# Modulation passes tied behind the linear attention's VectorE chain, and counted out anew

## The chip, the core and the metric

The kernel runs on one core of a Trainium2 chip. The metric is device time in microseconds of one execution. The engines are TensorE (PE in the profile, its weight loads PEld), VectorE (DVE), ScalarE (ACT), GpSimd (POOL) and SyncE (SP, whose DMA queue is SPq).

## What is computed

One step of a diffusion backbone with two layers over 512 latent and 128 context tokens (640 in all, 1,024 channels). Layer 0 mixes tokens with neighbourhood attention (A, 8 heads) beside bidirectional gated linear attention (B, 4 heads of key width 64 and value width 128), layer 1 with grouped-query attention; each layer ends in a gated feed-forward part. Every normalised input is scaled, shifted and gated by vectors of a modulation, one set for latent tokens and one for context tokens. The change lies in layer 0's mixer. Of the reference:

```python
def modulation(cvec, w, bias):
    mod = (jax.nn.silu(cvec) @ w + bias).reshape(-1, 1, 6 * D_MODEL)
    return jnp.split(mod, 6, axis=-1)

def gla_scan(q, k, v, g, s0):              # g = log alpha <= 0, chunks of tokens
    ...
    def step(s, inp):
        qc, kc, vc, gc = inp
        bcum = jnp.cumsum(gc.astype(jnp.float32), axis=2)
        o_inter = jnp.einsum('bhid,bhde->bhie', qc * jnp.exp(bcum).astype(qc.dtype), s)
        diff = bcum[:, :, :, None, :] - bcum[:, :, None, :, :]
        decay = jnp.exp(jnp.where(causal[:, :, None], diff, -jnp.inf)).astype(qc.dtype)
        att = jnp.einsum('bhid,bhjd,bhijd->bhij', qc, kc, decay)
        o = o_inter + jnp.einsum('bhij,bhje->bhie', att, vc)
        ...
        s_new = (jnp.exp(blast[:, :, 0, :])[..., None].astype(s.dtype) * s
                 + jnp.einsum('bhjd,bhje->bhde', k_dec, vc)).astype(s.dtype)
```

## The kernel before

Tokens lie along the free axis, channels along the partitions. A product of fp32 values is made of three matmuls over halves: a weight tile `ws` comes by DMA on SP's queue, its high half `wh` is a cast on ScalarE (L111), its low half `wl` a difference on VectorE or GpSimd (L112), and `step` (L155) multiplies `hh`, `hl` with `wh`, `wl` into `mm`; products with tokens on the partitions go into `tm` (L602 to L604), from which VectorE and ScalarE copy the values `v`. The `wh` pieces have six buffers.

Layer 0's mixer runs in this order on the chip: gates and scans of B, then the pieces of `ORDER` ("a0", "s0", "a1", "o0", "q0", "s1", "o1"), then A. Here 0 and 1 are the two pairs of heads, m in the code:

- "a" (`gla_scores`): decayed scores by levels. A level subtracts sums of gates into `ea` and `eb` (VectorE, L864 and L865), takes exponentials (ScalarE, L844), and multiplies by keys and queries (`ea` on GpSimd L870, `eb` on VectorE L871). 40 small matmuls (`lev`, L884) follow, which VectorE evicts through a mask (L889, into `acc` for the first of six levels; GpSimd adds the later ones to it). Two last levels go through `off` (L921), copied to `att` by ScalarE (L926, L927); eight VectorE copies (L930) put the diagonal blocks of `acc` into `att`.
- "s" (`gla_states`): decayed keys `kd` (ScalarE L948, GpSimd L949), transposed and copied to `kt`; `ds` (TensorE, L969), and the states `S` (VectorE, L974 and L975).
- "o" (`gla_out`): outputs `go` from `att`, `S` and decayed queries `qd`, copied to `got`.

Beside this, TensorE works through other products (values, the gate `rg`, A's first queries and keys), which `fill.some(n)` takes from a queue at fixed places. A's own keys of the context come as `kc` by DMA (SP, L801) and are split into `kch` (ScalarE) and `kcl` (VectorE); its first scores are `nas` (L1100).

The modulation's later vectors are made on VectorE from weights in `wa`: `modulations()` yields 48 steps in this stage, each a DMA of 256 KB into one of three `wa` buffers (SP, L323) and two multiply-and-add passes (L326, written to `junk` and, the second, over `wa` itself), 96 passes in all. `Fill.some(n, m)` also takes m of these steps. The numbers `SLEV`, `SOFF` and `SST` say how many are taken after a level, ahead of `off`, and ahead of each "s" and "o". An instruction's place on its engine is then set by a scheduler that builds one order for each engine; each engine works through its list in that order. `tc.issue_after(x)` is a condition on this order alone: what is issued within it stands behind x.

Of the kernel before, what the change touches and what calls it, by code (L numbers as in the profile page):

```python
# [12 lines left out]
ALU = mybir.AluOpType  # L13
# [7 lines left out]
NT = LAT + CTX  # L21
# [9 lines left out]
def kernel(ctx: ExitStack, tc: tile.TileContext, a: dict, o: dict):  # L31
# [205 lines left out]
    def run(gen):  # L237
        for _ in gen:
            pass

    class Fill:

# [17 lines left out]
        def some(self, n, m=0):  # L260
            while m and self.aside:
                m -= 1
                if next(self.aside[0], self) is self:
                    self.aside.pop(0)
            self.owed += n
            n = int(self.owed)
            self.owed -= n
            while n and self.queue:
                with tc.high_priority(offset=0):
                    end = next(self.queue[0], self) is self  # L270
                if end:
                    self.queue.pop(0)
                else:
                    n -= 1
                    self.newest = newest[0]
# [365 lines left out]
    def layer0(H, raws):  # L641
# [95 lines left out]
        for m, d in keys:  # L737
# [7 lines left out]
            last = nc.scalar.activation(ab, ab, AF.Exp, scale=-1.0)  # L745
            fill.some(RG1)
        with tc.issue_after(last.ins):
            for key in keys:
                last = nc.scalar.activation(logs[key], logs[key], AF.Ln, bias=1.0)
        for key in keys:  # L750
# [5 lines left out]
            else:  # L756
                nc.vector.tensor_tensor_scan(rev(c), gscan, rev(mins[key]), 0.0, ALU.mult, ALU.add)
            fill.some(RG2)


        with tc.issue_after(last.ins):
            S, OT, att = {}, {}, {}

            def piece(kind, m):
# [3 lines left out]
                elif kind == "s":  # L768
                    fill.until(g_vg)
                    fill.some(0, SST)  # L770
                    gla_states(m, kg[m], cum[m], vg, S, fill)
                elif kind == "o":
# [73 lines left out]
    def gla_scores(m, k, q, FG, fill):  # L846
        def level(h):
# [21 lines left out]
            if h > 1:  # L869
                nc.gpsimd.tensor_tensor(ea[:, 0:NT], ea[:, 0:NT], k[:, 0:NT], ALU.mult)  # L870
            nc.vector.tensor_tensor(eb[:, 0:NT], eb[:, 0:NT], q[:, 0:NT], ALU.mult)  # L871
            return ea, eb
# [51 lines left out]
        for e in range(2):  # L924
# [3 lines left out]
            for j in range(4):  # L928
                pj = slice(32 * j, 32 * j + 32)
                nc.vector.tensor_copy(  # L930
                    x[pj, 0:NT].rearrange("p (t i) -> p t i", i=128)[:, :, 32 * j:32 * j + 32],
# [5 lines left out]
    def gla_states(m, k, FG, vg, S, fill):  # L937
# [25 lines left out]
        for d, tiles in enumerate(order):  # L963
# [9 lines left out]
            for i, t in enumerate(tiles[0:3]):  # L973
                nc.vector.scalar_tensor_tensor(s[:, i + 1, :], s[:, i, :], dec[d][:, t:t + 1], ds[:, 128 * i:128 * i + 128], ALU.mult, ALU.add)  # L974
            nc.vector.tensor_copy(s[:, 4, :], ds[:, 384:512])  # L975
            nc.gpsimd.dma_start(o["gla"][d, m], s[:, 4, :])
# [536 lines left out]
RG1 = 6  # L1513
# [4 lines left out]
ROUT = 6  # L1518
SLEV = 2
SOFF = 4  # L1520
SST = 4
# [133 lines left out]
```

## Time and profile before

| | us |
|---|---|
| median of 3 runs | 1721.39 (1718.57 to 1723.66) |
| the profiled execution | 1717.48 |
| its span | 1715.7 |

TensorE is busy for 95% of the span, VectorE for 73%, ScalarE for 43% and GpSimd for 12%; TensorE's mean granted clock is 0.974 of full speed. Busy time is an average over stages: the first 260 us, in which layer 0's mixer makes B, look unlike the rest. Times below count from the span's start.

### The profile page before, as it was taken

Reading aid. Unit: us, or ns where it says so; the run is one execution under the profiler, and the core shown is the slowest. Engines: PE = TensorE matmul, PEld = TensorE weight load, DVE = VectorE, ACT = ScalarE, POOL = GpSimd, SP = SyncE. Lnnn points to the kernel's source line nnn. Section 1 sums busy time; section 2 is a strip of 40 time slices with the busy share of each in tenths; the row PEclk is TensorE's granted clock in tenths of the full one; section 3 lists DMA queues with packets and bytes.
Section 4 is the critical chain, followed back from the end, with each engine's and each line's share of the span. In section 5 each row is a group of like instructions: output and inputs, shape, how many; then the busy total and the mean of one; then the engine's idle time right before and its main releaser. Section 6 shows DMA issues by size and latency. Waiting matters only on the chain.

```text
span 1715.7 us, 33434 instructions
## 1 busy us (share of the span) xinstructions
PE 1635.8 (95%) x13142; PEld 1563.1 (91%) x13142; DVE 1258.2 (73%) x2767; ACT 742.4 (43%) x1681; POOL 208.9 (12%) x473
## 2 busy tenths in 40 slices
PE   7986988999999999999999999999999999999997
PEld 5886887879999999999998888889999999999997
DVE  5999865775999999986656987885876544663664
ACT  4443354453533323322335577775553322331342
POOL 2125541210200000000003310100100000000001
PEclk8998989999999999999998999999999999999999
DMA  8643332323354455453232200110222222222222
GB/s 320 206 136 103 103 103 81 95 87 105 100 163 155 146 174 184 146 158 110 72 122 88 69 20 14 50 56 31 70 82 79 62 76 75 81 71 82 73 70 68
DMA packets 68014, 175.22 MB, mean 102 GB/s; under 512 B 7920, under 2 KB 9744, under 8 KB 66832
## 3 DMA queue, kind: packets, MB, share of 16 engines
q1 hardware_dynamic: 67024, 171.48, 31.0%
q8 instruction: 103, 1.69, 0.4%
q0 software_dynamic: 832, 1.60, 0.3%
q14 instruction: 55, 0.45, 0.1%
HBM read 165.71 MB, written 7.34 MB: 101 GB/s over the span
## 4 chain that ended last, share of the span: by engine, by line
PE 79%; DVE 13%; ACT 3%; DMA 2%; issue 2%; POOL 1%; SPq 0%; ACTq 0%; DVEq 0%; POOLq 0%
PE mm L155 66%; DVE junk L326 2%; PE gpo L1339 2%; DVE wa L326 2%; PE gpt L1327 1%; DVE wl L112 1%; DMA wa<-in_ada_wt_dram 1%; PE gs L1318 1%; PE gs L1319 1%; DVE mx L1065 1%; PE ss L420 1%; PE tm L602 1%; PE napo L1131 1%; PE tm L604 1%; PE tm L603 1%
## 5 line engine op out<-in xcount | busy, mean ns | idle before, releaser
L155 PE MATMUL mm<-hh,wl 128*128 128x320 f32 x2080 | 652.3, 315 | 4.7 <-ACT rg L689 2.6
L155 PE MATMUL mm<-hl,wh 128*128 128x320 f32 x2080 | 648.2, 312 | 0.0
L155 PE MATMUL mm<-hh,wh 128*128 128x320 f32 x2080 | 641.5, 312 | 0.0
L111 ACT CAST wh<-ws 128x512 fp32r<-128x512 f32 x376 | 228.8, 615 | 438.2 <-PE mm L155 395.7
L155 PEld LDWEIGHTS mm<-hh,wl 128*128 128x128 f32 x2080 | 394.6, 190 | 14.7 <-issue 4.8
L155 PEld LDWEIGHTS mm<-hl,wh 128*128 128x128 f32 x2080 | 395.1, 190 | 2.6 <-issue 1.0
L155 PEld LDWEIGHTS mm<-hh,wh 128*128 128x128 f32 x2080 | 393.4, 190 | 0.4 <-issue 0.2
L112 DVE TENSOR_TENSOR wl<-ws,wh 128x512 fp32r<-128x512 f32 x348 | 243.5, 702 | 150.5 <-ACT wh L111 149.3
L155 PE MATMUL mm<-glo,wh 128*128 128x320 f32 x704 | 218.0, 310 | 0.0
L155 PE MATMUL mm<-ghi,wh 128*128 128x320 f32 x704 | 218.0, 311 | 0.0
L155 PE MATMUL mm<-ghi,wl 128*128 128x320 f32 x704 | 216.1, 311 | 0.0
L498 DVE SCALAR_TENSOR_TENSOR x<-mm,mod,x 128x192 f32<-128x192 f32 (+2 forms) x240 | 96.9, 435 | 88.8 <-PE mm L155 87.8
L155 PEld LDWEIGHTS mm<-ghi,wl 128*128 128x128 f32 x704 | 132.3, 189 | 1.3 <-issue 1.3
L155 PEld LDWEIGHTS mm<-glo,wh 128*128 128x128 f32 x704 | 133.1, 189 | 0.0
L155 PEld LDWEIGHTS mm<-ghi,wh 128*128 128x128 f32 x704 | 132.9, 189 | 0.1
L326 DVE SCALAR_TENSOR_TENSOR junk<-wa,sb 128x512 f32<-128x512 f32 x160 | 120.8, 760 | 7.2 <-DMA wa<-in_ada_wt_dram 6.9
L326 DVE SCALAR_TENSOR_TENSOR wa<-wa,sb 128x512 f32<-128x512 f32 x160 | 114.3, 721 | 0.3
L532 POOL MEMSET u<- 128x1 f32 x88 | 8.6, 100 | 760.9 <-DVE gate L525 426.3
L535 ACT COPY u<-mm 128x320 f32<-128x320 f32 x88 | 37.8, 431 | 87.7 <-PE mm L155 81.8
L602 PE MATMUL tm<-wl,hh 128*128 128x256 f32 x200 | 58.6, 300 | 8.0 <-ACT v L611 4.6
L1071 ACT ACTIVATE gp<-gs,mx,rq 128x640 f32<-128x640 f32 x64 | 57.1, 892 | 16.9 <-DVE mx L1067 11.6
L538 ACT COPY u<-mm 128x192 f32<-128x192 f32 x88 | 28.4, 323 | 79.7 <-PE mm L155 79.7
(302 smaller groups left out, 2436.6 us busy)
## 6 DMA issues: line engine op xcount, KB each, us to landing
ws<-in_wu_dram SPq DMA_DIRECT2D x88, 512.0 KB, 3.2
wa<-in_ada_wt_dram SPq DMA_DIRECT2D x160, 256.0 KB, 3.3
ws<-in_wd_dram SPq DMA_DIRECT2D x32, 448.0 KB, 3.5
aw<-in_ada_w_dram SPq DMA_DIRECT2D x8, 1024.0 KB, 14.7
ws<-in_w_ab_dram SPq DMA_DIRECT2D x16, 512.0 KB, 3.7
ws<-in_wd_dram SPq DMA_DIRECT2D x16, 512.0 KB, 3.5
x<-in_xT_dram SPq DMA_DIRECT2D x16, 320.0 KB, 3.0
ws<-in_w_gqa_dram SPq DMA_DIRECT2D x10, 512.0 KB
```

The lines of the kernel that those rows point to most:

```text
L111: nc.scalar.copy(hi, src)
L112: eng.tensor_tensor(lo, src, hi, ALU.subtract)
L155: newest[0] = nc.tensor.matmul(ps, x, y[:, s], start=st, stop=sp_).ins
L326: nc.vector.scalar_tensor_tensor(w if v else junk, w, 1.0, cs[v, j], ALU.mult, ALU.mult, accum_out=acc[:, k, v, j:j + 1])
L420: nc.tensor.matmul(ps[0:rows, c:c + 2], part[:, t], onesd, start=True, stop=True)
L498: nc.vector.scalar_tensor_tensor(x[:, b:e], ps[:, b - HN * h:e - HN * h], gate[:, v, m:m + 1], old[:, b:e], ALU.mult, ALU.add)
L535: nc.scalar.copy(u[:, 1:321], ps)
L538: nc.scalar.copy(u[:, 321:513], ps[:, 0:192])
L602: nc.tensor.matmul(ps, hh[:, s], wlo, start=(k == 0), stop=False)
L603: nc.tensor.matmul(ps, hl[:, s], whi, start=False, stop=False)
L1071: nc.scalar.activation(dst, src, AF.Exp, bias=mx[:, i:i + 1], accum_out=sm[:, i:i + 1], **kw)
L1339: last = nc.tensor.matmul(po[64 * f:64 * f + 64, 0:128], vs[t][:, 64 * kv:64 * kv + 64], mates[f]["x"][:, 128 * t:128 * t + 128], start=(t ...
```

## The change

Every step that `fill.some` takes from the aside list is now issued behind `anchor[0]`. The anchor is the latest of three kinds of VectorE instruction: a level's product `eb` with the queries, a copy into `att`, and the copy that ends a set of states. The numbers change as well: three steps beside each of the four gates (`SG1`) and two beside each of the four scans (`SG2`), 20 together, then one a level instead of two, two ahead of `off` instead of four, and the four of an "s" behind its states instead of ahead of them.

```diff
+    anchor = [None]
...
             while m and self.aside:
                 m -= 1
-                if next(self.aside[0], self) is self:
-                    self.aside.pop(0)
+                with ExitStack() as behind:
+                    if anchor[0] is not None:
+                        behind.enter_context(tc.issue_after(anchor[0].ins))
+                    if next(self.aside[0], self) is self:
+                        self.aside.pop(0)
...
-            fill.some(RG1)
+            fill.some(RG1, SG1)
...
-            fill.some(RG2)
+            fill.some(RG2, SG2)
...
                     fill.until(g_vg)
+                    gla_states(m, kg[m], cum[m], vg, S, fill)
                     fill.some(0, SST)
-                    gla_states(m, kg[m], cum[m], vg, S, fill)
...
-            nc.vector.tensor_tensor(eb[:, 0:NT], eb[:, 0:NT], q[:, 0:NT], ALU.mult)
+            anchor[0] = nc.vector.tensor_tensor(eb[:, 0:NT], eb[:, 0:NT], q[:, 0:NT], ALU.mult)
...
-                nc.vector.tensor_copy(
+                anchor[0] = nc.vector.tensor_copy(
                     x[pj, 0:NT].rearrange("p (t i) -> p t i", i=128)[:, :, 32 * j:32 * j + 32],
...
-            nc.vector.tensor_copy(s[:, 4, :], ds[:, 384:512])
+            anchor[0] = nc.vector.tensor_copy(s[:, 4, :], ds[:, 384:512])
...
-SLEV = 2
-SOFF = 4
+SG1 = 3
+SG2 = 2
+SLEV = 1
+SOFF = 2
 SST = 4
```

How many of the 96 passes stand ahead of these instructions in VectorE's order:

| ahead of | before | after |
|---|---|---|
| the first scan | 43 | 43 |
| the first `eb` that is taken from the sums, m = 0 | 47 | 44 |
| the first eviction of scores, m = 0 | 57 | 46 |
| the third | 63 | 52 |
| the sixth and last | 71 | 54 |
| the first copy into `att`, m = 0 | 79 | 58 |
| the last copy of states, m = 0 | 90 | 58 |
| the first eviction, m = 1 | 90 | 62 |
| the sixth | 90 | 78 |
| the first copy into `att`, m = 1 | 90 | 82 |
| the last copy of states, m = 1 | 96 | 90 |

**The first place: VectorE around the first eviction of scores (`acc<-lev`), m = 0.** `wl` with the higher number belongs to a later weight piece. Before:

```order
L326 SCALAR_TENSOR_TENSOR junk_2192,adacc_1699<-wa_2190,sb_767 128x512
L112 TENSOR_TENSOR wl_1333<-ws_1330,wh_1332 128x512
L609 COPY v_801<-tm_1085 128x256
L112 TENSOR_TENSOR wl_1579<-ws_1576,wh_1578 128x512
L326 SCALAR_TENSOR_TENSOR wa_2190,adacc_1699<-wa_2190,sb_773 128x512
L326 SCALAR_TENSOR_TENSOR junk_2286,adacc_1699<-wa_2284,sb_770 128x512
L326 SCALAR_TENSOR_TENSOR junk_2291,adacc_1699<-wa_2289,sb_767 128x512
L326 SCALAR_TENSOR_TENSOR wa_2284,adacc_1699<-wa_2284,sb_776 128x512
L889 TENSOR_TENSOR acc_1132<-lev_1180,mask32_112 128x320
L864 TENSOR_TENSOR ea_1254<-cum_788 128x640
```

After (the changed file's lines stand six further on):

```order
L877 TENSOR_TENSOR eb_1277<-eb_1277,kqg_654 128x640
L332 SCALAR_TENSOR_TENSOR junk_1325,adacc_1111<-wa_1323,sb_767 128x512
L332 SCALAR_TENSOR_TENSOR wa_1323,adacc_1111<-wa_1323,sb_773 128x512
L615 COPY v_816<-tm_1181 128x256
L112 TENSOR_TENSOR wl_1424<-ws_1421,wh_1423 128x512
L112 TENSOR_TENSOR wl_1655<-ws_1652,wh_1654 128x512
L112 TENSOR_TENSOR wl_1787<-ws_1784,wh_1786 128x512
L895 TENSOR_TENSOR acc_1238<-lev_1281,mask32_112 128x320
L870 TENSOR_TENSOR ea_1350<-cum_788 128x640
L871 TENSOR_TENSOR eb_1349<-cum_788 128x640
```

Four passes that stood right ahead of the eviction are gone from there, and three splits `wl` stand behind the copy of `v`; the last of them is of the seventh weight piece that is cast in this stretch, where there are six buffers for `wh`. On TensorE 38 instead of 15 groups of L155 stand ahead of the first `lev`.

**The second place: VectorE between the copies into `att` and the states of m = 0.** Before, from the copies on (the states end 13 rows further on):

```order
L930 COPY att_1812<-acc_1132 32x5x32 x4
L930 COPY att_1819<-acc_1132 32x5x32 x4
L326 SCALAR_TENSOR_TENSOR junk_2749,adacc_2510<-wa_2747,sb_767 128x512
L326 SCALAR_TENSOR_TENSOR wa_2742,adacc_2510<-wa_2742,sb_776 128x512
L326 SCALAR_TENSOR_TENSOR junk_2794,adacc_2510<-wa_2792,sb_770 128x512
L871 TENSOR_TENSOR eb_2039<-eb_2039,kqg_739 128x640
L326 SCALAR_TENSOR_TENSOR wa_2747,adacc_2510<-wa_2747,sb_773 128x512
L112 TENSOR_TENSOR wl_2298<-ws_2295,wh_2297 128x512
L326 SCALAR_TENSOR_TENSOR wa_2792,adacc_2510<-wa_2792,sb_776 128x512
L326 SCALAR_TENSOR_TENSOR junk_2799,adacc_2510<-wa_2797,sb_767 128x512
L326 SCALAR_TENSOR_TENSOR wa_2797,adacc_2510<-wa_2797,sb_773 128x512
L326 SCALAR_TENSOR_TENSOR junk_2804,adacc_2510<-wa_2802,sb_770 128x512
```

After:

```order
L871 TENSOR_TENSOR eb_2100<-cum_789 128x640
L936 COPY att_1872<-acc_1238 32x5x32 x4
L936 COPY att_1879<-acc_1238 32x5x32 x4
L877 TENSOR_TENSOR eb_2100<-eb_2100,kqg_739 128x640
L112 TENSOR_TENSOR wl_2344<-ws_2341,wh_2343 128x512
L980 SCALAR_TENSOR_TENSOR S_1955<-S_1955,dec_1888,ds_1946 128x128 x3
L981 COPY S_1955<-ds_1946 128x128
L980 SCALAR_TENSOR_TENSOR S_1983<-S_1983,dec_1899,ds_1974 128x128 x3
L981 COPY S_1983<-ds_1974 128x128
L332 SCALAR_TENSOR_TENSOR junk_2037,adacc_1111<-wa_2035,sb_770 128x512
```

All passes have left the stretch between `att` and the last copy of `S`, where eleven stood; the products and subtractions of `eb` are level 0 of m = 1.

**The third place: ScalarE behind the copies into `att`, m = 1.** Before:

```order
L844 ACTIVATE qd_2752<-cum_788 128x640
L844 ACTIVATE qd_2755<-cum_788 128x640
L632 ACTIVATE qx_2899<-mm_2851 128x5x4x16
L948 ACTIVATE kd_2812<-cum_789,to_2813 128x128 x5
L948 ACTIVATE kd_2823<-cum_789,to_2824 128x128 x5
L111 CAST kch_3084<-kc_3086 128x512
L111 CAST kch_3084<-kc_3090 128x512
L844 ACTIVATE qd_2959<-cum_789 128x640
L1000 COPY got_2772<-go_2758 128x512
L1001 COPY got_2772<-go_2758 128x128
L844 ACTIVATE qd_2962<-cum_789 128x640
```

After:

```order
L850 ACTIVATE qd_2772<-cum_788 128x640
L850 ACTIVATE qd_2775<-cum_788 128x640
L954 ACTIVATE kd_2812<-cum_789,to_2813 128x128 x5
L954 ACTIVATE kd_2823<-cum_789,to_2824 128x128 x5
L1006 COPY got_2792<-go_2778 128x512
L1007 COPY got_2792<-go_2778 128x128
L638 ACTIVATE qx_2899<-mm_2851 128x5x4x16
L850 ACTIVATE qd_2959<-cum_789 128x640
L850 ACTIVATE qd_2962<-cum_789 128x640
```

The two casts `kch` have left this stretch and stand behind both copies `got` of the last output; on VectorE their counterpart `kcl` stands behind the second `kl` of A's first heads, and on SP the loads `kc` behind the eight loads `vw`, `vc` and the first weights of A.

## Rows read from the trace of the kernel before

**Rows 1.** The page: span, and busy time of each engine with its share of the span and its instructions.

```profile
span 1715.7 us, 33434 instructions
...
PE 1635.8 (95%) x13142; PEld 1563.1 (91%) x13142; DVE 1258.2 (73%) x2767; ACT 742.4 (43%) x1681; POOL 208.9 (12%) x473
```

**Rows 2.** The chain of waits within 0 to 420 us, share of that time by engine and line.

```profile
by line: PE mm L155 22.5%; DVE junk L326 8.5%; DVE wa L326 6.2%; DMA wa<-in_ada_wt_dram 5.5%; issue 4.6%; DVE wl L112 2.9%; PE napo L1131 2.7%; DVE eb L865 2.3%; DMA x<-in_xT_dram 2.2%; PE ada L296 2.0%; DVE ea L864 1.9%; DVE eb L871 1.8%; 
```

**Rows 3.** Busy time of each engine by stretch: stretch and length in us, then PE, PEld, DVE, ACT and POOL (each with its instructions), the granted clock, the DMA engines' share and GB/s. The first stretch runs from the first level's `eb` (m = 0) to the first eviction of scores; the second ends with the third eviction, the third with the sixth; the fourth ends with the states of m = 0, the fifth with the start of the `att` copies of m = 1 and the sixth with the states' matmuls of m = 1.

```profile
110.14:121.95 11.81, 10.98 (x185) 10.33 (x184) 11.81 (x28) 3.91 (x8) 3.27 (x2) 1.00 0.47 150
121.95:141.56 19.61, 14.31 (x299) 13.46 (x274) 19.61 (x28) 7.55 (x13) 11.08 (x6) 0.75 0.25 79
141.56:161.55 19.99, 12.81 (x263) 11.68 (x261) 19.99 (x36) 6.20 (x11) 11.30 (x7) 0.99 0.38 117
161.55:188.08 26.53, 23.20 (x308) 21.92 (x309) 22.91 (x62) 8.16 (x22) 7.42 (x5) 0.84 0.42 135
188.08:223.94 35.86, 34.63 (x709) 31.97 (x709) 29.71 (x31) 15.18 (x28) 25.18 (x16) 0.93 0.27 86
223.94:248.36 24.42, 20.85 (x148) 18.83 (x146) 16.45 (x33) 17.76 (x38) 13.01 (x8) 0.79 0.28 91
```

**Rows 4.** Groups of VectorE's instructions between 50 and 240 us: the two kinds of pass (busy us, mean ns, idle us before them and what ended most of it).

```profile
L326 DVE SCALAR_TENSOR_TENSOR junk<-wa,sb 128x512 f32<-128x512 f32 x48 | 43.3, 911 | 5.0 <-DMA wa<-in_ada_wt_dram 4.7
L326 DVE SCALAR_TENSOR_TENSOR wa<-wa,sb 128x512 f32<-128x512 f32 x48 | 37.9, 805 | 0.2
```

**Rows 5.** VectorE's timeline, m = 0: start and duration in us.

```profile
121.33 0.68 DVE L326 SCALAR_TENSOR_TENSOR wa<-wa,sb 128x512 f32<-128x512 f32 x1
...
121.95 0.48 DVE L889 TENSOR_TENSOR acc<-lev,mask 128x320 f32<-128x320 f32 x1
...
132.09 1.75 DVE L326 SCALAR_TENSOR_TENSOR junk<-wa,sb 128x512 f32<-128x512 f32 x1
...
141.56 0.48 DVE L889 TENSOR_TENSOR acc<-lev,mask 128x320 f32<-128x320 f32 x1
...
149.77 1.63 DVE L112 TENSOR_TENSOR wl<-ws,wh 128x512 fp32r<-128x512 f32 x1
...
157.88 1.33 DVE L112 TENSOR_TENSOR wl<-ws,wh 128x512 fp32r<-128x512 f32 x1
...
159.14 1.88 DVE L871 TENSOR_TENSOR eb<-eb,kqg 128x640 f32<-128x640 f32 x1
...
161.55 0.48 DVE L889 TENSOR_TENSOR acc<-lev,mask 128x320 f32<-128x320 f32 x1
```

**Rows 6.** TensorE's timeline beside it (four rows) and one of ScalarE: start, duration, and in brackets the idle time before and what ended it.

```profile
114.44 0.28 PE L603 MATMUL tm<-wh,hl 128*128 128x256 f32 x1
...
114.56 0.28 PE L604 MATMUL tm<-wh,hh 128*128 128x256 f32 x1
...
114.68 0.31 PE L155 MATMUL mm<-hh,wl 128*128 128x320 f32 x1
...
114.83 0.31 PE L155 MATMUL mm<-hl,wh 128*128 128x320 f32 x1
...
112.74 2.81 ACT L111 CAST wh<-ws 128x512 fp32r<-128x512 f32 x4 [0.34 <-PE tm L604]
```

**Rows 7.** VectorE's waits between 50 and 240 us: in total, times, the longest.

```profile
DVE junk L326 <- DMA wa<-in_ada_wt_dram: 4.7, 6, 1.6
...
DVE att L930 <- ACT att L927: 2.6, 1, 2.6
...
DVE eb L871 <- ACT eb L844: 2.6, 3, 0.9
```

**Rows 8.** The stretch behind the last level of m = 0: the passes (L326) alone in it, as in rows 3 but for VectorE only (a pass counts two instructions, the second an accumulator read), then VectorE's copies into `att`, its last copy of states, and TensorE's second group of `ds`.

```profile
161.55:188.08 26.53, 16.03 (x40) 0.84 0.42 135
...
172.83 2.58 DVE L930 COPY att<-acc 32x160 f32<-32x160 f32 x8
...
187.79 0.29 DVE L975 COPY S<-ds 128x128 f32<-128x128 f32 x1
...
178.56 1.09 PE L969 MATMUL ds<-v,kt 128*64 128x128 f32 x16
```

**Rows 9.** VectorE's timeline, m = 1: the start of two levels without passes in between, and the copies into `att`.

```profile
204.99 0.82 DVE L864 TENSOR_TENSOR ea<-cum 128x640 f32<-128x640 f32 x1
...
210.28 0.81 DVE L864 TENSOR_TENSOR ea<-cum 128x640 f32<-128x640 f32 x1
...
223.94 2.60 DVE L930 COPY att<-acc 32x160 f32<-32x160 f32 x8 [2.63 <-ACT att L927]
```

**Rows 10.** ScalarE's casts of the context keys, TensorE's `ds` of m = 1 and the first scores of A.

```profile
232.86 0.62 ACT L111 CAST kch<-kc 128x512 fp32r<-128x512 f32 x1 [3.75 <-DMA kc<-in_na_kc_dram]
...
235.58 0.62 ACT L111 CAST kch<-kc 128x512 fp32r<-128x512 f32 x1 [2.10 <-DMA kc<-in_na_kc_dram]
...
245.26 3.10 PE L969 MATMUL ds<-v,kt 128*64 128x128 f32 x32
...
260.76 0.36 PE L1100 MATMUL nas<-kk,q 128*128 128x256 f32 x1 [1.30 <-ACT kk L708]
```

## Prediction made before the changed kernel was run

> **What bounds the kernel now.** Over the span TensorE is busy for 95%, and VectorE for 73% [rows 1]; by that a shift of work on VectorE would be worth nothing. The chain of waits of the first 420 us says otherwise: beside 22.5% for matmuls it runs for 8.5 and 6.2% through the two kinds of modulation pass and for 5.5% through the passes' weight loads [rows 2]. The reader is to see there that the passes themselves, whose results nobody needs in this stage, are links of the chain. The stretches tell where. From the first level's `eb` to the sixth eviction (110.14 to 161.55) VectorE is busy all the time (11.81, 19.61 and 19.99 of as many us) while TensorE idles for 0.8, 5.3 and 7.2 us [rows 3]. In the next stretch, to the states of m = 0, VectorE idles for 3.6 us and TensorE for 3.3; in m = 1 TensorE idles for only 1.2 of 35.86 us and VectorE for 6.2 [rows 3]. So in m = 0 VectorE sets the pace, in m = 1 it has some room, and TensorE's whole idle time from 110.14 to 223.94 is 17.9 us, about the most that this stage can give, besides 3.6 in the tail [rows 3].
>
> **The price of a pass.** The two kinds took 911 and 805 ns on average, 81.2 us for 96 of them [rows 4], 0.85 us each. Back to back with nothing beside them they start 0.62 us apart (121.33 to 121.95), and one at 132.09 took 1.75 [rows 5]. I take 0.62 us for a pass that is moved: the surplus comes while GpSimd multiplies (11.08 of 19.61 us in that stretch [rows 3]), and when the pass is gone GpSimd's multiplication is still there and stretches the chain's own two-input instructions. The ends are 0.62 and 0.85.
>
> [...]
>
> **The change, by stretches.** All passes stay; 43 stand ahead of the first scan before and after. What differs is where the other 53 stand.
>
> *A, to the first eviction (121.95).* Eleven passes fewer stand ahead of it, 11 x 0.62 = 6.8 us. But VectorE's list now has a `v` copy and three splits `wl` directly ahead of it, the last of the seventh weight piece, whose cast needs one of six buffers back. With three passes fewer before it, `eb` starts some 1.9 us before 110.14, at about 108.3, and the copy of `v` that releases TensorE ends near 109.5. Then TensorE has two more token tiles of 24 matmuls 0.12 us apart (5.8 us) and 35 matmuls of L155 0.15 us apart (5.1 us) to do before the first weight piece is free [rows 6]: 120.4. A cast is 2.81 / 4 = 0.7 us [rows 6], a split about as long: 121.8. So the eviction comes when it came, and VectorE idles for some 7 us there. A = 0, with -6.8 (no wait) and +3 (a few more of TensorE's products ahead) as its ends.
>
> *B, to the third eviction.* Six passes before and after: 0.
>
> *C, to the sixth.* Two passes instead of eight: 6 x 0.62 = 3.7 us. Two splits (1.63 and 1.33 us, with the rows behind them some 2.8 us) stand earlier, in A's idle time, and a multiplication of 1.88 us behind the eviction instead of ahead [rows 5]: 8.3 in all, of 20.0 us. Three levels without passes in m = 1 take 5.29 us each (204.99 to 210.28 [rows 9]), 15.9 us. C = -8, ends -10 and -4.
>
> *D, to the last copy of states (188.08).* Twenty passes stand here, 16.0 us of the 26.5 [rows 8], where four remain; most of the 4.7 us of waits for `wa` [rows 7] lie here too, between the passes that go. VectorE alone would need some 9 us less than TensorE, which has its `ds` done at 179.65 (178.56 + 1.09) before [rows 8], 18.1 us after the sixth eviction. On top come the second states, 1.3 us. So the states are next late for `ds`: 19.4 instead of 26.5 us, D = -7, with 4 us of new idle time on VectorE. Ends -12 (the `ds` come sooner too, as the multiplications of `kd` do) and -4.
>
> Sum to the states of m = 0: -15, at about 173.
>
> *E, to the copies into `att` of m = 1 (223.94).* Here 24 passes come in, where none stood: 24 x 0.62 = 14.9 us, with the modulation's small sums 1.0 more. VectorE had 6.2 us of idle time in it, of which 2.6 is the wait for `att` by ScalarE and 2.6 for exponentials [rows 7]; I let 3 be filled. E = +13, ends +10 and +16. The `att` copies start 2 us sooner, at about 222.
>
> *F, the tail to the states of m = 1.* ScalarE stood for 3.75 and 2.10 us for the context keys' loads and cast them for 0.62 each, with the exponentials, `kt` and `ds` (245.26) queued behind it [rows 10]. With the casts moved behind the outputs, these 7.1 us leave the chain, but eight passes instead of six stand before the states, and GpSimd's 13 us [rows 3] stay. F = -5, ends -6.5 and 0.
>
> *G, the start of A.* The casts, their splits on VectorE and the loads behind eight others now stand just ahead of the first `nas` (260.76, which waited 1.30 us for `kk` [rows 10]). Two casts and two splits are 2.8 us, half hidden behind the heads' own products: +1.5, ends 0 and +5.
>
> Sum: -2 - 5 + 1.5 = -5.5, say -6 us. Against the profiled 1717.48 us that is 1711.5; the profiled execution lies 3.9 us under the median of the runs shown, so against that, 1721.39, it is **1715**. Adding all the ends on one side gives -22 or +17, which will not all come together.
>
> **Rivals.**
>
> *The debt is paid back in full.* From 110.14 to 223.94 VectorE was busy for 104.0 of 113.8 us [rows 3]. Only five passes, 3.1 us, leave this stretch (43 before, 38 after); all else is order. If the waits of A and D are as long as the idle time of before, 9.8 us, the `att` copies of m = 1 come where they came. The tail gains at most its waits, and the loads of context keys cost that again in front of A. Then nothing is left: 1719 to 1723. For it speaks that 7 + 4 us of new idle time stand against 9.8 us of old; against it that ScalarE's two waits of the tail are on the way to `ds`.
>
> *A larger gain.* If the weight piece in A is not on time's edge (a buffer free sooner, the `ws` load early), A gives its 6.8, and if `kd` and `ds` of m = 0 follow the earlier evictions, D gives 4 more: -17 us, 1704. For it speaks that TensorE was idle for 17.9 us in all these stretches [rows 3]; against it that the order names the waits.
>
> *Slower: the passes meet GpSimd in m = 1.* GpSimd is busy for 25.18 of 35.86 us there, for 11 of some 20 in m = 0 [rows 3]. The 24 passes come just into this. A pass beside GpSimd took 1.13 us more (1.75 against 0.62 [rows 5]); if ten of the 24 do, and the levels wait for that, E is 11 us longer and the sum +5.5: 1727. From five or six such passes on the gain is gone. For it speaks the busy GpSimd; against it that an instruction of the chain was stretched by the same neighbour already, and that TensorE has 34.6 us of work in this stretch [rows 3] to go on with.
>
> *The context keys come late.* SP's queue runs in order; the loads `kc` now wait behind ten others and behind values that must be stored first. If the first `nas` waits for them by as much as ScalarE did before, 5.9 us [rows 10], the sum is +0: 1721. It joins the first rival.
>
> **How the numbers follow.** The forecast, 1709 to 1720 with its own bounds, has 0.40; the larger gain 0.13; no gain, by repayment or by late context keys, 0.30; slower through GpSimd 0.17. About 0.3% (5.2 us, 1716.2 to 1726.6) is what a measurement of this kernel tells from no change. The forecast lies on its lower edge, so a part of its chance (0.05 or more) falls into "same", as does a little of the last. Faster 0.48, same 0.35, slower 0.17. The range that holds the time 8 times in 10 runs from 1704, the larger gain, to 1728, just past the slower rival.
>
> **What would show it.** Right: VectorE idles from about 115 to 121 and the first eviction stays near 122; the sixth comes near 153.5; the states of m = 0 wait for `ds` and end near 173; the `att` copies of m = 1 start near 222; no ScalarE wait for context keys ahead of `kd`, `ds` of m = 1 near 239; the first `nas` near 255. The passes in m = 1 near 0.65 us on average. Wrong: a first eviction before 117 (the larger gain); passes of over 1 us in m = 1 and `att` later than 226 (GpSimd); a first `nas` that waits for a context key; or a gain at the first `nas` that is gone by 300 us, since TensorE's other products, put off until then, would have to be done anyway.

## The result, and the profile of the changed kernel

The changed kernel is slower: 1736.71 us (median of 4 runs, 1735.61 to 1738.19) against 1720.14, ratio 1.0097 with a 95% interval of 1.0085 to 1.0110. The profiled run took 1736.35 us. Its page begins:

```profile
span 1734.5 us, 33447 instructions
...
PE 1634.6 (94%) x13142; PEld 1562.3 (90%) x13142; DVE 1258.6 (73%) x2767; ACT 741.3 (43%) x1681; POOL 207.5 (12%) x473
```

VectorE's and TensorE's busy times are those of before [rows 1] within 1.2 us, so the 18.8 us between the two spans are idle time. The stretches of rows 3 in the changed kernel (same columns), ending with the first, third and sixth eviction, the states of m = 0, the `att` copies of m = 1 and its last copy of states; the last row is a stretch that the kernel before doesn't have:

```profile
108.66:123.83 15.17, 13.82 (x167) 13.59 (x168) 6.34 (x12) 4.68 (x10) 2.65 (x2) 0.89 0.28 89
123.83:144.54 20.71, 15.79 (x316) 15.18 (x317) 20.71 (x27) 7.79 (x14) 13.20 (x7) 0.84 0.11 35
144.54:156.57 12.03, 7.53 (x192) 7.15 (x190) 11.27 (x17) 3.56 (x6) 8.07 (x5) 0.86 0.33 115
156.57:175.77 19.20, 19.00 (x269) 17.67 (x274) 13.97 (x31) 9.71 (x27) 8.54 (x6) 1.00 0.30 98
175.77:224.33 48.56, 38.94 (x818) 36.96 (x818) 46.46 (x83) 14.85 (x28) 22.99 (x16) 0.89 0.36 117
224.33:246.12 21.79, 19.55 (x165) 17.85 (x164) 19.84 (x37) 16.42 (x36) 13.78 (x9) 1.00 0.40 117
255.30:274.80 19.50, 0.00 (x0) 0.00 (x0) 3.54 (x8) 3.02 (x6) 1.43 (x2) 0.62 0.41 118
```

The reader is to see in the last row that TensorE does nothing for 19.5 us at the start of A, and in the others that the first five stretches together come out 2.4 us above the forecast: the `att` copies of m = 1 start at 224.33, where about 222 was forecast. VectorE's timeline at their ends (start, duration, idle time before and what ended it):

```profile
123.22 0.69 DVE L112 TENSOR_TENSOR wl<-ws,wh 128x512 fp32r<-128x512 f32 x1 [4.66 <-ACT wh L111]
...
123.83 0.48 DVE L895 TENSOR_TENSOR acc<-lev,mask 128x320 f32<-128x320 f32 x1
...
156.57 0.49 DVE L895 TENSOR_TENSOR acc<-lev,mask 128x320 f32<-128x320 f32 x1 [0.76 <-POOL acc L897]
...
172.75 1.11 DVE L980 SCALAR_TENSOR_TENSOR S<-S,dec,ds 128x128 f32<-128x128 f32 x3 [3.69 <-PE ds L975]
...
224.33 2.60 DVE L936 COPY att<-acc 32x160 f32<-32x160 f32 x8 [0.18 <-ACT att L933]
...
247.26 0.69 DVE L332 SCALAR_TENSOR_TENSOR junk<-wa,sb 128x512 f32<-128x512 f32 x1
```

At 123.22 the split of the seventh weight piece starts, for which VectorE has waited 4.66 us; at 156.57 the sixth eviction comes 5.0 us sooner than before [rows 5]; at 172.75 the states wait for `ds`; at 224.33 m = 1 copies into `att`, 0.4 us later than before [rows 9]; at 247.26 the last junk is written. What ended the empty stretch stands on three queues, after TensorE's `ds` of m = 1: SP's DMA queue (three rows), ScalarE, TensorE:

```profile
239.58 1.97 PE L975 MATMUL ds<-v,kt 128*64 128x128 f32 x32 [0.35 <-ACT kt L966]
...
241.36 13.38 SPq L800 DMA_DIRECT2D vw<-values  x5
...
254.84 2.46 SPq L802 DMA_DIRECT2D vc<-in_na_vc_dram  x1
...
257.99 1.05 SPq L807 DMA_DIRECT2D kc<-in_na_kc_dram  x2
...
270.55 1.26 ACT L111 CAST kch<-kc 128x512 fp32r<-128x512 f32 x2 [19.90 <-DMA kc<-in_na_kc_dram]
...
274.89 0.55 PE L1106 MATMUL nas<-kk,q 128*128 128x256 f32 x1 [19.59 <-DVE kk L716]
...
276.39 0.47 PE L155 MATMUL mm<-hl,wh 128*128 128x320 f32 x1
...
276.65 0.47 PE L155 MATMUL mm<-hh,wh 128*128 128x320 f32 x1
```

SP issues the last five `vw` loads in the 13.4 us after 241.36 (8.4 us of them are waits for TensorE and ScalarE), then `vc`, a weight piece, and at 257.99 the context keys `kc`; they land 12.5 us later, ScalarE has waited 19.90 us for them, and `kk`, queued behind their splits, lets the first `nas` start at 274.89 instead of 260.76 [rows 10]. The matmuls behind it start 0.27 us apart instead of 0.15 [rows 6]: the granted clock is 0.50 from 274.8 to 280.4; from there to 285 it is 1.00, and they start 0.15 us apart again.

To see where time is lost, take the n-th of the 8,352 matmuls of L155 in each trace and subtract its start in the kernel before (us; plus is later). Within the first mixer the products' order differs a little between kernels; from 318 us on it does not matter. Each row is one execution, the profiled one, which can lie some us off the median of its kernel: that of `before` lies 2.7 us below the 1720.14, that of `after_vw16` 4.8 us below its own 1716.64, that of `s_ahead_kc_early` 4.9 us above its own 1731.17.

| at, in the kernel before | 251 | 318 | 897 | 1042 | end |
|---|---|---|---|---|---|
| changed | -6.8 | +15.4 | +16.3 | +18.9 | +18.9 |
| junk_ring | -13.6 | -3.7 | +15.5 | +17.1 | +18.4 |
| kc_early | -7.0 | +0.6 | +1.4 | +3.6 | +3.8 |
| before_kc_early | -2.7 | -1.8 | -1.9 | -1.7 | 0.0 |
| before_kc_late | -0.7 | +9.6 | +10.6 | +13.3 | +13.3 |
| tie_old | +24.2 | +38.7 | +38.6 | +38.8 | +40.5 |
| s_ahead | +19.0 | +17.5 | +17.4 | +17.9 | +19.2 |
| s_ahead_kc_early | +10.5 | +11.8 | +13.2 | +18.6 | +18.6 |
| after_vw16 | -4.8 | -4.8 | -3.9 | -5.1 | -5.2 |
| fill4 | -12.8 | -2.0 | -2.6 | +4.3 | +4.3 |
| fill3 | -10.6 | +9.9 | +10.0 | +9.8 | +9.7 |
| fill5 | -11.3 | -2.6 | -2.3 | -3.7 | -3.8 |
| fill5_vw16 | -11.6 | -8.2 | -6.5 | -8.0 | -7.7 |

So the change does put TensorE some 7 us ahead, loses 22 us at the start of A, and 2.6 more at the start of layer 1.

### The profile page after: what moved, and what is told of

Read it like the earlier page. It is cut to its first block, busy times and chain, and to the rows that moved or that the text cites. A ratio compares the mean times of both kernels' runs of the same rounds, so it can differ in the third digit from the quotient of the medians.

```text
span 1734.5 us, 33447 instructions
## 1 busy us (share of the span) xinstructions
PE 1634.6 (94%) x13142; PEld 1562.3 (90%) x13142; DVE 1258.6 (73%) x2767; ACT 741.3 (43%) x1681; POOL 207.5 (12%) x473
## 4 chain that ended last, share of the span: by engine, by line
PE 79%; DVE 12%; ACT 3%; DMA 2%; issue 2%; POOL 1%; SPq 1%; ACTq 0%; DVEq 0%; POOLq 0%
PE mm L155 67%; PE gpo L1345 2%; PE gpt L1333 2%; PE gs L1324 1%; DVE junk L332 1%; DVE wa L332 1%; PE gs L1325 1%; DMA wa<-in_ada_wt_dram 1%; DVE wl L112 1%; DVE eb L871 1%; PE ss L426 1%; DMA kc<-in_na_kc_dram 1%; DVE ea L870 1%; DVE mx L1071 1%; PE napo L1137 1%
## 5 line engine op out<-in xcount | busy, mean ns | idle before, releaser
L155 PE MATMUL mm<-hh,wl 128*128 128x320 f32 x2080 | 651.8, 315 | 3.6 <-DVE kl L715 2.3
L155 PE MATMUL mm<-hl,wh 128*128 128x320 f32 x2080 | 647.8, 312 | 0.2 <-DVE hl L472 0.2
L155 PE MATMUL mm<-hh,wh 128*128 128x320 f32 x2080 | 642.0, 312 | 0.0
L155 PEld LDWEIGHTS mm<-hh,wl 128*128 128x128 f32 x2080 | 395.3, 190 | 13.0 <-issue 6.7
L155 PEld LDWEIGHTS mm<-hl,wh 128*128 128x128 f32 x2080 | 395.6, 190 | 3.1 <-DVE h L461 1.2
L155 PEld LDWEIGHTS mm<-hh,wh 128*128 128x128 f32 x2080 | 393.8, 190 | 0.4 <-issue 0.2
L112 DVE TENSOR_TENSOR wl<-ws,wh 128x512 fp32r<-128x512 f32 x348 | 237.7, 685 | 150.4 <-ACT wh L111 149.2
L155 PE MATMUL mm<-glo,wh 128*128 128x320 f32 x704 | 217.7, 310 | 0.0
L155 PE MATMUL mm<-ghi,wh 128*128 128x320 f32 x704 | 217.7, 310 | 0.0
L155 PE MATMUL mm<-ghi,wl 128*128 128x320 f32 x704 | 215.8, 310 | 0.0
L155 PEld LDWEIGHTS mm<-ghi,wl 128*128 128x128 f32 x704 | 132.3, 189 | 1.3 <-issue 1.3
L155 PEld LDWEIGHTS mm<-glo,wh 128*128 128x128 f32 x704 | 133.0, 189 | 0.0
L155 PEld LDWEIGHTS mm<-ghi,wh 128*128 128x128 f32 x704 | 132.8, 189 | 0.1
L1071 DVE TENSOR_REDUCE mx<-gs 128x1 f32<-128x640 f32 x64 | 52.5, 820 | 14.8 <-PE gs L1325 14.3
```

The source lines that it names most:

```text
L112: eng.tensor_tensor(lo, src, hi, ALU.subtract)
L155: newest[0] = nc.tensor.matmul(ps, x, y[:, s], start=st, stop=sp_).ins
L1071: nc.vector.tensor_reduce(mx[:, 0:n], s, axis, ALU.max, negate=True)
```

## Experiments

Theory 1 is the late load of the context keys, theory 2 my rival of passes stretched beside GpSimd in m = 1. All ratios are to runs of the kernel before made beside the kernel in question, with their 95% interval.

**Tie or numbers.** `no_tie` leaves the tie out of the changed kernel; `tie_old` is the kernel before with the tie alone.

```diff
-                    if anchor[0] is not None:
+                    if False:
```

> The changed kernel without the tie: the new numbers and places alone. The order of VectorE's passes is that of the kernel before at each milestone (57 ahead of the first eviction, 90 ahead of the states of m = 0). Theory 1 and theory 2 both: the time of before within 0.3%, 1716 to 1725. If it is as slow as the changed kernel, the numbers and not the tie are the cause.

> The kernel before with the tie alone: old numbers, the steps of an "s" ahead of the states. Now nothing is taken beside the gates, and 10 instead of 57 passes stand ahead of the first eviction; the debt stands behind the levels, and the last passes behind the att copies of m = 1, with six more after the states. Theory 1: kc stands behind all vw loads and vc again, and it is as slow as the changed kernel or slower: 1735 to 1755. If only the number of passes in m = 1 counted (theory 2), 26 passes between the first eviction and att of m = 1 (44 to 69) against 20 (62 to 82) would make it slower by some 4 us than the changed kernel, without a wait for kc.

Measured: `no_tie` 1718.78 us, 1.0001 (0.9992 to 1.0011); `tie_old` 1758.03, 1.0226 (1.0210 to 1.0241). The numbers alone move nothing, since without the tie the scheduler draws the passes forward all the same (57 of them ahead of the first eviction, as before); the tie alone costs most. In `tie_old` ScalarE waits 13.9 us for `kc` until 286.07, but TensorE is 24.2 us late at 251 us already, ahead of that wait: the late keys are only a part of its loss.

**The junk's ring.** `junk` and `kc` take their buffers from one ring of three, so `kc` follows the last passes.

```diff
-                    junk = N("junk")[:, 0:512]
+                    junk = np_.tile([P, NT], F32, tag="nq", name="junk", bufs=2)[:, 0:512]
```

> The changed kernel, but the passes' junk output goes to another ring of two buffers instead of the ring of three that the context keys kc also use; passes, tie and numbers as in the changed kernel. Theory 1 (the loss is the late kc load: its buffer comes free only after the last passes, which are now tied behind the states of m = 1, and SP's order puts it behind nine other loads): kc is issued before 235 us, ScalarE has no wait of 19.9 us for it, the first nas starts near 256 instead of 274.9, and the time falls by 17 to 20 us to about 1718. Theory 2 (the passes in m = 1, stretched beside GpSimd, cost the time): the att copies of m = 1 stay at 224 and the time stays at 1733 to 1738.

Measured: 1733.16 us, 1.0083 (1.0068 to 1.0098): the total went nearly nowhere, and by the total theory 1 was refuted. The rows of SP, ScalarE and TensorE, and a wait of ScalarE at 425 to 470 us, say otherwise:

```profile
222.87 0.58 SPq L807 DMA_DIRECT2D kc<-in_na_kc_dram  x1
...
228.37 0.62 ACT L111 CAST kch<-kc 128x512 fp32r<-128x512 f32 x1 [1.78 <-DMA kc<-in_na_kc_dram]
...
258.88 0.39 PE L1106 MATMUL nas<-kk,q 128*128 128x256 f32 x1
...
ACT hh L463 <- DVE h L461: 22.8, 6, 13.9
```

`kc` goes out at 222.87, the first `nas` starts at 258.88, and TensorE is 3.7 us ahead at 318 us. Then it loses some 17 us by 450 us, in the next norm, where ScalarE waits 13.9 us for `h` on VectorE. A second effect of the edit hid the first (the changed kernel and `kc_early`, whose passes keep their ring, lose no more than 1.6 us there); only the table by stretches told them apart. With `kc` in the ring of A's bias tiles instead (`kc_early`), the passes' ring is left alone.

```diff
-            kc, x, y = N("kc")[:, 0:512], *(...)
+            kc, x, y = T("kc", "bias", n=512, bufs=NBI), *(...)
```

> The changed kernel with the context keys kc in two buffers of the ring that A's bias tiles use later, so that no pass's junk stands in their way and the passes' own ring is untouched; kc is loaded far ahead (31st on SP's queue). Theory 1 (the late kc is the whole loss at A's start, and the run with junk in another ring lost its time again because junk then shared a ring with the squares of the next norm): the first nas near 256, TensorE 4 us ahead of the kernel before at 300 to 400 us and still so at 450, total 1714 to 1721, no more than 0.2% above before. If TensorE is ahead at 400 but falls back by 15 us at 430 us again, that second loss is not the junk ring's.

> The kernel before with kc in the bias ring, nothing else. ScalarE's waits of 3.75 and 2.10 us for kc at 229 and 233 us go. Theory 1: TensorE is 3 to 5 us ahead of the kernel before at 300 us, total 1713 to 1718. If it is the same as before, those waits were covered and my term for the tail (5 us) was no gain of the change either.

Measured: `kc_early` 1721.02, 1.0012 (1.0001 to 1.0023), so all but 0.12 of the 0.97% went with the late keys. `before_kc_early` 1718.44, 0.9997 (0.9988 to 1.0005). Its `ds` and first `nas` of TensorE:

```profile
241.88 3.68 PE L969 MATMUL ds<-v,kt 128*64 128x128 f32 x32 [0.36 <-ACT kt L960]
...
257.96 0.36 PE L1100 MATMUL nas<-kk,q 128*128 128x256 f32 x1 [1.18 <-ACT kk L708]
```

Without ScalarE's waits for `kc` in the tail [rows 10] `ds` is done 2.8 us sooner (245.56 instead of 248.36), not the 5 of my term F; 1.9 us of it are left at 897, and nothing at the end. In `kc_early` the lead of 7 us at 251 us is still spent by the first `nas` (TensorE's rows, then two stretches as in rows 3):

```profile
247.47 0.46 PE L1003 MATMUL go<-qd,S 64*128 64x128 f32 x2 [2.36 <-DVE S L980]
...
260.69 0.36 PE L1106 MATMUL nas<-kk,q 128*128 128x256 f32 x1 [1.47 <-ACT kk L714]
...
250.00:255.00 5.00, 5.00 (x61) 4.76 (x59) 3.75 (x14) 1.93 (x5) 1.13 (x2) 0.50 0.26 99
...
255.00:260.00 5.00, 4.22 (x18) 3.96 (x17) 0.98 (x2) 1.36 (x3) 0.00 (x0) 0.65 0.37 134
```

TensorE waits 2.36 us for the states of m = 1, and runs at a granted clock of 0.50 and 0.65 in ten us in which the kernel before had 1.00 (its own two stretches below); the first `nas` comes when it came before, although no key is late.

```profile
250.00:255.00 5.00, 5.00 (x66) 4.79 (x65) 3.07 (x8) 1.59 (x4) 1.67 (x3) 1.00 0.32 118
...
255.00:260.00 5.00, 4.46 (x44) 4.04 (x42) 1.08 (x3) 2.05 (x5) 0.00 (x0) 1.00 0.74 199
```

**The place on SP alone.** `before_kc_late` moves no pass; it only puts `kc` behind `vc`.

```diff
+            with tc.issue_after(behind_vc.ins):
                 nc.sync.dma_start(kc, ...)
```

> The kernel before, all its passes where they were, with one condition: the two loads of context keys stand behind vc on SP, as the changed kernel's order has them. Theory 1 (the place of kc on SP is the loss): kc goes out at 254 to 256 us and lands 8 to 12 us later, the first nas moves from 260.8 to 268 to 275, and the time rises by 8 to 17 us to 1727 to 1736 with no pass moved. If the passes are needed for the loss, it stays within 0.3% of before.

Measured: 1729.99, 1.0073 (1.0051 to 1.0095).

```profile
253.03 1.18 SPq L802 DMA_DIRECT2D kc<-in_na_kc_dram  x2
...
265.34 0.62 ACT L111 CAST kch<-kc 128x512 fp32r<-128x512 f32 x1 [11.39 <-DMA kc<-in_na_kc_dram]
...
270.20 0.55 PE L1101 MATMUL nas<-kk,q 128*128 128x256 f32 x1 [11.53 <-DVE kk L710]
```

Issued at 253.03, used 12 us later, `nas` 9.4 us late: the place on the queue costs by itself. `kc_pool` is the complement: the ring as in the changed kernel, but the load on GpSimd's queue.

> The changed kernel with kc in the ring of the junk as it was, but loaded by GpSimd's queue instead of SP's, where it stands behind the copies out of the states. It tells the buffer from the queue: the last junk is written at 247.3 to 247.9 us, so kc could go out at 248 instead of 258. If the ten us on SP's queue and the transfer of 12.5 us behind the vw, vc and ws loads make the loss, the first nas comes at 255 to 260 and the total is 1717 to 1724; if the buffer's release alone does, the first nas stays after 268.

Measured: 1721.42, 1.0014 (1.0004 to 1.0024).

```profile
249.64 0.69 DVE L332 SCALAR_TENSOR_TENSOR junk<-wa,sb 128x512 f32<-128x512 f32 x1
...
256.12 0.62 ACT L111 CAST kch<-kc 128x512 fp32r<-128x512 f32 x1 [3.08 <-DMA kc<-in_na_kc_dram]
...
260.44 0.36 PE L1106 MATMUL nas<-kk,q 128*128 128x256 f32 x1 [1.47 <-ACT kk L714]
```

The last junk is written at 249.64, as late as ever, and `kc` is there at 256.1: the wait for the buffer is not what costs, its place on SP's queue is.

**The four steps behind the states.** `s_ahead` takes them ahead of the states again; `s_ahead_kc_early` adds the early keys.

> The changed kernel with one part undone: the four steps of an "s" are taken ahead of its states again, so that the last passes are tied behind the att copies of m = 1 and not behind its states. Theory 1: the last junk is read some 8 us earlier, kc goes out in front of the last five vw loads, and most of the loss comes back: 1716 to 1722. Theory 2 (passes in m = 1): as many passes stand in m = 1 or just behind it, so the time stays above 1730.

> The run with the four steps ahead of the states, with kc in the bias ring. Theory 1: its wait of 13.1 us for kc, with kcl and the states of m = 1 (258.99) queued behind it, goes; from 1738 to 1715 to 1722. If it stays above 1730, the place of the steps costs by itself.

Measured: 1738.20, 1.0106 (1.0081 to 1.0130), and 1731.17, 1.0064 (1.0048 to 1.0079). I expected recovery and was wrong: `kc` went out at 244 us but ScalarE still waited 13.1 us for it, until 256.10, now with `kcl` and the states queued behind. With early keys, 1731.17 lies above the 1730 that I had named: the place of the steps costs by itself, since this kernel differs from `kc_early` (0.12% above before) in nothing else. TensorE is 10.5 us behind at 251 us there, ahead of A. Which wait does it was not followed up.

**How wide the vw loads are.** Each `vw` load is four grid rows by 32 columns. In the changed kernel's DMA (245 to 271 us, 40 slices of 0.65 us; the first row is the share of the 16 DMA engines that is busy, in tenths) the rate sits near 100 GB/s while they run:

```profile
DMA  4223322222232222222389999999222222222220
GB/s 142 104 98 139 136 95 101 101 107 104 98 117 98 98 98 98 98 98 98 104 180 375 252 268 224 246 271 240 82 98 101 98 98 98 101 98 101 98 76 13
...
kc<-in_na_kc_dram SPq DMA_DIRECT2D x2, 256.0 KB, 12.5
```

The reader is to see three parts: a share of about a quarter at 98 GB/s until 258, then 0.9 or more for some 5 us when `vc`, the weight piece and `kc` have been issued, then again a quarter at 98 GB/s until `kc` has landed at 270.5, though no other load was issued after 259.

```diff
-                nc.sync.dma_start(v, grid[4 * t:4 * t + 4, c0:c0 + 32, :])
+                for i in range(4):
+                    nc.sync.dma_start(v[32 * i:32 * i + 32, :], grid[4 * t + i, c0:c0 + 32, :])
```

> The changed kernel with each of the eight vw loads (four grid rows by 32 columns) written as four loads of one row; kc stays behind all of them and vc on SP. In the changed kernel the vw loads move at about 100 GB/s with a mean busy share of 0.2 to 0.3 of the 16 DMA engines, and kc takes 12.5 us to land behind them. If they run on a quarter of the engines only, and kc's part on those engines waits for the rest of them, loads of 32 whole rows spread over all engines: the stretch from the last vw issue to kc's landing is shorter by 5 us or more, the first nas comes at 262 to 270 instead of 274.9, and the total is 1722 to 1732. If the time lies with the wait for vw's buffers on SP alone (13.4 us), kc is issued at 258 or later and the total stays at 1734 to 1739.

> The kernel before with the same split of the vw loads. kc stood ahead of the last five there and landed in 2 to 3 us, so no more than the ws behind vc can come sooner: within 0.3% of before (1715 to 1724); layer 1's ScalarE order is one of its own here, which may move it by up to 3 us either way.

Measured: the changed kernel with it 1716.64, 0.9991 (0.9976 to 1.0007); the kernel before with it 1718.68, 0.9995 (0.9984 to 1.0006). SP, ScalarE, TensorE, and issues with the median us to landing:

```profile
238.31 16.10 SPq L801 DMA_DIRECT2D vw<-values  x32
...
254.98 0.85 SPq L808 DMA_DIRECT2D kc<-in_na_kc_dram  x2
...
259.20 0.62 ACT L111 CAST kch<-kc 128x512 fp32r<-128x512 f32 x1 [0.53 <-DMA kc<-in_na_kc_dram]
...
259.16 0.36 PE L1107 MATMUL nas<-kk,q 128*128 128x256 f32 x1 [1.02 <-DVE kk L716]
...
vw<-values SPq DMA_DIRECT2D x29, 64.0 KB, 1.9
...
kc<-in_na_kc_dram SPq DMA_DIRECT2D x2, 256.0 KB, 3.4
```

`kc` stands where it stood, behind all `vw` and `vc`, and is issued only 3 us sooner; but it lands in 3.4 us instead of 12.5, and all the loss is gone. In the profiled execution TensorE keeps a lead of 5 us to the end, but that execution was the fastest of ten: by the medians 2.4 us are gained, and the interval still holds 1.

**The rest: VectorE's new idle time and layer 1.** The fill kernels take extra steps beside the second level of m = 0, where VectorE idles, and fewer behind `att` of m = 1, all with early keys: 4, 7, 3 and 5 extra, then 0, 0, 0 and 1 ahead of the outputs of m = 0 (which stand behind `att` of m = 1), and 4, 0, 4 and 4 behind the states, as far as any are left (3, 0, 4 and 1).

```diff
-            fill.some(RLEV, SLEV)
+            fill.some(RLEV, SLEV + (5 if m == 0 and li == 1 else 0))
```

> The changed kernel with kc early, and four steps (eight passes) taken beside the second level of m = 0 instead of ahead of the second outputs. It asks whether VectorE's idle time ahead of the first eviction (115 to 123 us) takes eight passes for nothing: then the first eviction stays within 1.5 us of 123.8 while att and the states of m = 1 come as before, and the stretch from att to the states of m = 1, where eight passes took 11.9 us, is shorter by up to 5 us. Theory 1: total 1714 to 1720. If those passes delay the first eviction by 0.62 us each, 1720 to 1725.

> As fill4, with seven steps (fourteen passes) beside the second level of m = 0 and none left behind att of m = 1. Behind the states of m = 1 VectorE has only A's own work, so TensorE's wait of 2.4 us for them and the six passes ahead of the first kl go: total 1712 to 1719. If fourteen passes overfill the idle time ahead of the first eviction (about 12 fit), the first eviction comes 2 to 4 us later and the total is that of fill4 or above.

> As fill4, but with three steps beside the second level of m = 0 and four behind the states of m = 1. In the changed kernel and in all runs that lost 2.6 us or more at the start of layer 1 (900 to 990 us), ScalarE's order there differs from that of the kernel before (34 lines); in this one it is that of the kernel before again. If that order is the second loss, TensorE's lead at 890 us (2 to 4 us) is kept to the end and the total is 1714 to 1718, faster than before. If the loss comes from something else (times of arrival, the clock), TensorE falls back by 2.6 us or more at 930 to 980 us here too.

> As fill3, with five steps beside the second level of m = 0, one ahead of the second outputs and one behind the states of m = 1; layer 1's order is that of the kernel before here too. Lead at 890 us 1 to 4 us (ten passes fit into the idle time ahead of the first eviction), kept to the end: 1714 to 1718. If six passes behind the states of m = 1 and not their place ahead of the first eviction set the start of A, fill5 is ahead of fill3 by 1 to 3 us.

> fill5 with the same split. In fill5 the ws behind vc lands after 9.5 us (median) and ScalarE waits 1.9 us for it. If the narrow vw loads are what slows it, 1709 to 1713; if layer 1's order (its own here) costs 2 us or more, 1713 to 1718.

Measured: `fill4` 1719.68, 1.0004 (0.9994 to 1.0014); `fill7` 1724.16, 1.0024 (1.0012 to 1.0037); `fill3` 1726.43, 1.0036 (1.0023 to 1.0050); `fill5` **1712.55, 0.9957 (0.9942 to 0.9972)**; `fill5_vw16`, with the `vw` loads split as above, **1709.18, 0.9946 (0.9932 to 0.9961)**. These two are faster than both kernels, by 0.4 and 0.5% against the one before. Eight and ten passes in the idle time left the first eviction at 122.9 and 124.5 (`kc_early`, with none: 124.6); fourteen moved it to 125.9. `fill3` lost on the same queue in another load (SP, VectorE, TensorE):

```profile
260.45 0.39 SPq L329 DMA_DIRECT2D wa<-in_ada_wt_dram  x1
...
271.92 0.69 DVE L332 SCALAR_TENSOR_TENSOR junk<-wa,sb 128x512 f32<-128x512 f32 x1 [12.39 <-DMA wa<-in_ada_wt_dram]
...
273.65 0.55 PE L1106 MATMUL nas<-kk,q 128*128 128x256 f32 x1 [11.57 <-DVE kk L716]
```

The last pass's weights are issued behind `vw` and `vc` at 260.45, VectorE waits 12.39 us for them with A's `kl` queued behind the pass, and a later `nas` for 11.57. In `fill5`, where two passes instead of eight stand between `att` and the states of m = 1 and two instead of six behind these, the first `nas` comes 6.8 us sooner than in `kc_early`:

```profile
span 1711.9 us, 33447 instructions
...
253.90 0.39 PE L1106 MATMUL nas<-kk,q 128*128 128x256 f32 x1
```

Layer 1's loss goes with ScalarE's order there. The six kernels with the changed kernel's order (itself, `kc_early`, `s_ahead_kc_early`, `kc_pool`, `before_kc_late`, `fill4`) lose 2.2 to 6.9 us between 897 and 1042 us; the six others with the order of before (`no_tie`, `tie_old`, `s_ahead`, `before_kc_early`, `fill7`, `fill3`) between -0.2 and +0.5; each number is of one execution. `junk_ring`, with a third order, loses 1.6. The longest wait of TensorE there in the changed kernel is one that the kernel before does not have (whose own waits there are others, of 2.7 us and less):

```profile
PE gs L1324 <- ACT gp L1077: 4.2, 1, 4.2
```

`before_kc_late` shows the same wait without any pass moved. That this order alone costs the time was not tried by an edit in layer 1 and is not shown.

## Why the prediction was wrong, step by step

The steps on the passes held within 2.2 us each; the one on A's start (G) did not, and it decided. The ends of the range were also added up wrongly: all on one side they give -25.3 and +16, not -22 and +17, and the sum of the table, +18.9, lies above both.

| step | predicted | measured |
|---|---|---|
| A, first eviction | 0 (stays near 122) | +1.9 (123.83), VectorE idle there |
| B | 0 | +1.1 (20.71 us for 19.61) |
| C | -8 | -8.0 (12.03) |
| D | -7, at `ds` | -7.3 (19.20), waiting 3.69 for `ds` |
| E | +13 | +12.7 (48.56) |
| F, `att` to `ds` of m = 1 | -5 | -7.2 (17.2 us, from 24.4) |
| G, `ds` to the first `nas` | +1.5, ends 0 and +5 | **+20.9** (33.3 us, from 12.4) |
| behind it | none | +1.3 by 318, +0.9 by 897, +2.6 in layer 1 |

**G.** I named the kernel's new order (the loads of the context keys behind eight `vw`, `vc` and a weight piece), but priced it with the work of the casts, and its rival with ScalarE's old waits of 3.75 and 2.10 us [rows 10]. Those waits belong to a load that stood ahead of all eight `vw` on SP (`kc` at 230.34 and 232.91, the first `vw` at 233.28), as SP's queue in the kernel before shows:

```profile
230.34 0.33 SPq L801 DMA_DIRECT2D kc<-in_na_kc_dram  x1
...
232.91 0.33 SPq L801 DMA_DIRECT2D kc<-in_na_kc_dram  x1
...
233.28 1.83 SPq L794 DMA_DIRECT2D vw<-values  x3
```

Moved behind the others, the load cost their issue and a longer transfer: SP needed until 257.99 to get there, 13.4 us of it for five `vw` (8.4 of them in waits for TensorE and ScalarE), and the loads landed after 12.5 us, where before ScalarE's casts began 2.5 and 2.7 us after the issues [rows 10]. The sign that I had named for this, a first `nas` that waits for a context key, is what came. A second mistake lies under it: I did not ask why the scheduler had moved the loads. The tie puts the last passes behind the states, their `junk` holds the ring that `kc` needs, and so the scheduler placed `kc` late; `junk_ring` shows this, since another ring alone brought `kc` to 222.87. Of the 20.9 us, 14.2 are the keys: with them early (`kc_early`) the first `nas` starts at 260.69. The other 6.7 are the lead itself, spent ahead of `nas`: in `kc_early` TensorE waits for the states and runs at a lower clock there. G had no term for that either; only the first rival had.

**E** and **F** came near by luck. In E the 24 passes took 19.1 us and not 14.9, but VectorE's three splits of weights there took 2.0 us instead of 4.8, and 4.1 us of its idle time were filled instead of 3. In F the two waits for keys, which I took for the gain, are worth 2.8 us at `ds` (`before_kc_early`). Of the other 4.4 us, 1.1 are `ds` itself (1.97 us instead of 3.10, in a stretch with a granted clock of 1.00 instead of 0.79); what the rest was stays open.

**The rivals.** GpSimd in m = 1 was not it. The 24 passes there took 19.1 us for 48 records, 0.80 us each against my 0.62, and three of them, not ten, were stretched to over 1 us (1.76 to 2.05); the stretch came out at 48.56 us for a forecast of 48.9. A pass did take longer beside GpSimd, as in the rows of before (1.75 us against 0.62 [rows 5]): of the eight passes between `att` and the states of m = 1, the five that began while GpSimd multiplied took 1.74 to 2.05 us, and the three that began while it did not took 0.68 or 0.69. The late context keys were a rival, at a quarter of their price and counted as "no change". The repayment that I gave 0.30 is there too: `kc_early` leads by 7 us at 251 us and ends 0.1% above before. With the `vw` loads split (`after_vw16`) the changed kernel ran in 1716.64 us, near the 1715 forecast, but only 2.4 us below the kernel before beside it, where 6 were forecast: the queue was the largest term left out, not the only one.

## What to carry to other kernels

When a change reorders work, read the DMA queue's order as closely as the engines', and price a load that moves by what is issued, waited for and transferred ahead of it there, not by the waits that it had at its old place. A buffer ring that two users share ties them together, also through the scheduler's order: look who allocates behind the instruction that you delay. And split a loss by stretches before believing a total; `junk_ring` cured its cause and showed the same time.

## What the runs showed of the hardware

A load of 256 KB (`kc`) landed after 12.5 us behind five `vw` loads of four blocks each, and after 3.4 us behind the same bytes in loads of 32 rows (`after_vw16`). From 250 to 256 us, among the first kind, the changed kernel's DMA engines moved 101 GB/s at a mean busy share of 0.27 of the 16; from 246 to 252 us, among the second, those of `after_vw16` moved 162 GB/s at 0.58. Which engines carried a load is not shown: no row here names them one by one. That `kc` waited for its part on just the engines that the `vw` loads kept busy is my estimate, from the stretch before `kc` had landed (263 to 270.5 us), which ran at 0.26 and 96 GB/s, the same share and rate, though no other load was issued then.
